# One transformer layer on one core: third to eighth row pairs also loaded with features first, and both input projections fed by sums and differences of the two row blocks

## Chip, cores and metric

One NeuronCore of one Trainium2 chip runs the whole program. The metric is the device time of one execution in microseconds (us). Time before: 2068.4 us, the median of 3 runs (2067.24 to 2069.75).

## What is computed

Two sequences (prompt and sample, 1024 rows of 1024 features, float32) pass through one encoder layer:

```python
mod = silu(c) @ w_ada + b_ada                 # shift, scale and gate, twice
h = rmsnorm(x, g_mix) * (1 + sc1) + sh1
z = h @ w_in                                  # 256 + 128 + 64 latents, 512 Fourier inputs
mla = attention(latents(z))                   # low-rank queries, keys, values
four = real(fft2(z[..., 448:])) @ w_four      # over rows and over 64 channels
x = x + ga1 * (concat(mla, four) @ w_out)
h2 = rmsnorm(x, g_ffn) * (1 + sc2) + sh2
x = x + ga2 * ((silu(h2 @ w_gate) * (h2 @ w_up)) @ w_down)
y = rmsnorm(x, g_final)
```

## The kernel before

Every float32 product is made of three matmuls. The helper `split` (L62 to L64) makes a rounded high part on ACT (L63, a cast) and the rest on DVE (L64, a subtraction); `mm3` (L78 to L81) multiplies high by high, high by low and low by high into one bank of PSUM.

The part that changes is the first stage and the transform stage behind it. The first stage goes through eight **row pairs**, four for each sequence; here they are counted from first to eighth (`k` = 0 to 7 in the code). A pair is two blocks of 128 rows, row block u = 0 and u = 1. The rows are stored so that row t of one block and of the other mirror each other in the Fourier transform over the rows. For each pair the program does this:

- `norm` loads the rows (tile `xt`, one row in each partition), sums their squares on ACT (L358, tile `junk`), takes 1/sqrt with six small POOL instructions (`rstd`, L102 to L109, tile `rs_r`), and scales the rows on DVE (L361).
- `flip` transposes 16 blocks of 128x128 on PE (L374), two chunks of features at a time, scales and shifts the result on its way out of PSUM (ACT, L381, tile `hf`, features in the partitions), and splits it into `hh` and `hl`.
- `zproj` (one for each row block) projects to the 448 latents, 24 matmuls with 448 columns from `hh`, `hl`; it then takes two more squares and `rstd`, applies the rotation (POOL adds, L426) and the norms (DVE, L427, L428), and stores the key part (`kv` to `ckv_d`). `latents` transposes the result (4 on PE, L442), splits it into `lh`, `ll` and stores these (`lat_d`).
- `evenodd` makes the sum and the difference of the two blocks on POOL (L396, tile `eo`) and splits them into `eoh`, `eol`. `fourier_in` multiplies these with weights into which the channel transform is folded (`wcs`, 280 and 256 columns), 24 matmuls each, and folds the results into `zc` and `zs`.

The order is written by hand: `pair(k)` runs both `zproj`, with the transposes of the next pair between them, then both `fourier_in` with the `latents` between, then `evenodd` of the next pair. The generator `extras` puts in one step at each `next(more)`: first eight chunks of the gate modulation (`wada`, 1 MB each, two buffers; 8 matmuls with 512 columns, L214), later the product of the output and Fourier weights (`wo4`, `lw`, L303), which goes to `wm_d` and `wn_d`. Each engine works through its queue in order, SyncE (SP) too, from whose queue all loads and stores here are issued: a store that waits for its data holds up the loads behind it.

The transform stage (`dft`, then `fourier_out`) splits the cosine and sine tables (`raw` to `tb`), `zc`, `zs` and the weights (`wraw` to `wm`, `wnr` to `wn`), multiplies, and stores to `fo_d`. It starts with `dft(0)`, for which the eighth pair of the first stage must be done. In between, chunks of the second modulation run (`mod2`). Attention and the FFN stand behind it and take most of the time.

## Time and profile before

| what | value |
|---|---|
| median of 3 runs | 2068.4 us |
| profiled execution, own time | 2068.6 us |
| its span in the profile | 2066.8 us |
| PE busy | 2018.9 us, 98% of the span |
| DVE, ACT, POOL busy | 68%, 43%, 41% |
| first pair's first projection starts | 51.1 us |
| second pair's projection starts | 75.1 us |
| transform stage: first `dft` matmul | 232.1 us |
| attention: first score matmul | 316.6 us |

The profile is of one execution. Times are counted from the span's start. "PE bank L81 <- DVE hl L64" in the view of waits means that a matmul of line 81 stood still until that DVE instruction ended. In the timeline a row has start, length, engine, line, operation, names of tiles, shapes and the number of instructions merged, and in brackets the idle time ahead of it. A matmul's length runs over into its successor (they are pipelined), so a matmul's price is read from one start to the next.

### The profile page before, as it was taken

Reading aid. Unit: us, or ns where it says so; the run is one execution under the profiler, and the core shown is the slowest. Engines: PE = TensorE matmul, PEld = TensorE weight load, DVE = VectorE, ACT = ScalarE, POOL = GpSimd, SP = SyncE. Lnnn points to the kernel's source line nnn. Section 1 sums busy time; section 2 is a strip of 40 time slices with the busy share of each in tenths; the row PEclk is TensorE's granted clock in tenths of the full one; section 3 lists DMA queues with packets and bytes.
Section 4 is the critical chain, followed back from the end, with each engine's and each line's share of the span. In section 5 each row is a group of like instructions: output and inputs, shape, how many; then the busy total and the mean of one; then the engine's idle time right before and its main releaser. Section 6 shows DMA issues by size and latency. Waiting matters only on the chain.

```text
span 2066.8 us, 28651 instructions
## 1 busy us (share of the span) xinstructions
PE 2018.9 (98%) x9994; PEld 1652.4 (80%) x9994; DVE 1406.0 (68%) x2078; ACT 898.4 (43%) x1753; POOL 841.4 (41%) x1014
## 2 busy tenths in 40 slices
PE   7899999999999999999999999999999999999998
PEld 4688778888888877888888888877788888888876
DVE  4567757766776778777777676778665665667685
ACT  2655535555555564232323355454333323336441
POOL 0555412111313227778778510333554454420142
PEclk9999999999999999999999999999999999999999
DMA  9675784533644375545545587665322222258662
GB/s 389 210 252 169 240 296 149 143 87 88 169 122 134 128 256 188 202 154 194 192 150 208 168 283 253 219 237 176 118 97 102 100 105 102 87 176 280 223 227 98
DMA packets 182685, 370.36 MB, mean 179 GB/s; under 512 B 18412, under 2 KB 57964, under 8 KB 179468
## 3 DMA queue, kind: packets, MB, share of 16 engines
q1 hardware_dynamic: 165196, 315.04, 45.0%
q0 software_dynamic: 17344, 53.49, 8.7%
q8 instruction: 78, 1.28, 0.3%
q14 instruction: 67, 0.55, 0.1%
HBM read 256.46 MB, written 120.39 MB: 182 GB/s over the span
## 4 chain that ended last, share of the span: by engine, by line
PE 55%; DVE 3%; DMA 2%; ACT 1%; POOL 1%; issue 1%; SPq 0%; DVEq 0%; ACTq 0%; POOLq 0%
PE bank L81 18%; PE bank L79 18%; PE bank L80 18%; DVE wl L64 1%; DMA draw<-t_d 1%; ACT wh L63 1%; DVE val L137 1%; DVE val L1599 0%; DMA val<-x_d 0%; DMA X<-hc_d 0%; DVE val L134 0%; DMA rgu<-in_wgu_dram 0%; DMA ga<-ga_d 0%; DMA draw<-s_d 0%; POOL rs_y L105 0%
## 5 line engine op out<-in xcount | busy, mean ns | idle before, releaser
L79 PE MATMUL bank<-H,wh 128*128 128x512 f32 x1232 | 487.6, 396 | 3.8 <-DVE val L137 1.9
L81 PE MATMUL bank<-H,wl 128*128 128x512 f32 x1232 | 488.4, 397 | 0.2 <-DVE wl L64 0.2
L80 PE MATMUL bank<-H,wh 128*128 128x512 f32 x1232 | 484.5, 393 | 0.3 <-DVE H L64 0.3
L79 PEld LDWEIGHTS bank<-H,wh 128*128 128x128 f32 x1232 | 231.3, 188 | 60.0 <-DVE val L137 2.8
L80 PEld LDWEIGHTS bank<-H,wh 128*128 128x128 f32 x1232 | 231.3, 188 | 57.9 <-DVE H L64 0.6
L81 PEld LDWEIGHTS bank<-H,wl 128*128 128x128 f32 x1232 | 231.3, 188 | 57.1 <-DVE wl L64 0.5
L64 DVE TENSOR_TENSOR wl<-draw,wh 128x512 fp32r<-128x512 f32 x286 | 201.9, 739 | 82.6 <-ACT wh L63 79.5
L137 DVE TENSOR_TENSOR val<-bank,val 128x512 f32<-128x512 f32 x200 | 136.6, 689 | 157.1 <-PE bank L81 151.6
L63 ACT CAST wh<-draw 128x512 fp32r<-128x512 f32 x286 | 168.8, 620 | 158.0 <-PE bank L80 91.4
L137 POOL TENSOR_TENSOR val<-val 128x512 f32<-128x512 f32 x58 | 83.5, 1447 | 367.0 <-DVE val L1573 189.2
L80 PE MATMUL bank<-wl,wh 128*128 128x512 f32 x572 | 223.7, 391 | 2.6 <-DVE wl L64 2.6
L63 ACT CAST wh<-rgu 128x512 fp32r<-128x512 f32 x172 | 106.8, 621 | 270.3 <-PE bank L80 210.8
L79 PE MATMUL bank<-wh 128*128 128x512 f32 x572 | 222.6, 389 | 0.0
L81 PE MATMUL bank<-wh,wl 128*128 128x512 f32 x572 | 222.6, 389 | 0.0
L63 ACT CAST wh<-val 128x512 fp32r<-128x512 f32 x133 | 82.3, 621 | 268.7 <-PE bank L80 249.2
L64 DVE TENSOR_TENSOR wl<-val,wh 128x512 fp32r<-128x512 f32 x133 | 133.5, 1005 | 78.1 <-ACT wh L63 77.9
L64 DVE TENSOR_TENSOR wl<-rgu,wh 128x512 fp32r<-128x512 f32 x172 | 164.3, 955 | 5.2 <-ACT wh L63 5.2
L134 POOL TENSOR_TENSOR val<-rgu 128x512 f32<-128x512 f32 x80 | 117.8, 1473 | 101.8 <-DMA rgu<-in_wgu_dram 98.0
L80 PEld LDWEIGHTS bank<-wl,wh 128*128 128x128 f32 x572 | 107.3, 188 | 28.6 <-DVE wl L64 6.4
L79 PEld LDWEIGHTS bank<-wh 128*128 128x128 f32 x572 | 107.4, 188 | 22.4
L81 PEld LDWEIGHTS bank<-wh,wl 128*128 128x128 f32 x572 | 107.4, 188 | 21.9
L1042 DVE TENSOR_REDUCE mx<-ps_s 128x1 f32<-128x1024 f32 x64 | 78.1, 1221 | 61.7 <-PE ps_s L1037 61.4
(356 smaller groups left out, 4113.0 us busy)
## 6 DMA issues: line engine op xcount, KB each, us to landing
rgu<-in_wgu_dram SPq DMA_DIRECT2D x86, 512.0 KB
draw<-s_d SPq DMA_DIRECT2D x143, 256.0 KB
s_d<-val POOLq DMA_DIRECT2D x88, 256.0 KB, 4.1
draw<-t_d SPq DMA_DIRECT2D x88, 256.0 KB
s_d<-val SPq DMA_DIRECT2D x66, 256.0 KB
draw<-in_w_down_dram SPq DMA_DIRECT2D x55, 256.0 KB
wada<-in_w_ada_dram SPq DMA_DIRECT2D x11, 1024.0 KB
xt<-in_x_dram SPq DMA_DIRECT2D x16, 512.0 KB
```

Of the source, the lines that this page charges most:

```text
L63: here["a"] = nc.scalar.copy(hi, src).ins
L64: here["v"] = nc.vector.tensor_tensor(out=lo, in0=src, in1=rd(hi), op=ALU.subtract).ins
L79: nc.tensor.matmul(out, lh, rh, start=first, stop=False, skip_group_check=cont)
L80: nc.tensor.matmul(out, lh, rl, start=False, stop=False, skip_group_check=cont)
L81: here["t"] = nc.tensor.matmul(out, ll, rh, start=False, stop=last, skip_group_check=cont).ins
L134: return eng.tensor_tensor(out=out, in0=x, in1=y, op=ALU.subtract).ins
L137: eng.tensor_tensor(out=out, in0=x, in1=y, op=ALU.add)
L1042: nc.vector.tensor_reduce(out=mx, in_=ps, axis=AX.X, op=ALU.max)
```

## The change

- `x` is also passed in transposed on the host (`xt0`, `xt1`: features first, 1 MB for each pair). From the third pair on this copy is loaded (`xT`) and the 16 transposes fall away. The rows are still loaded, for the squares alone; they are not scaled any more. In `scale_t` PE transposes the two columns `rs_r`, spread over 128 columns, so that a bank holds 1/sqrt along the free axis (2 transposes a pair); DVE multiplies `xT` with this bank (4 instructions of 128x512), and ACT scales and shifts in place (8 of 128x256).
- From the second pair on the latents use the same sum and difference as the Fourier inputs: `zboth` multiplies `eoh`, `eol` with the latent weights (48 matmuls with 448 columns, as before), and half the sum and half the difference of the two results are the two row blocks (one ACT copy, two DVE instructions). `hh`, `hl` and their splits fall away but for the first pair. The difference overwrites half of `hf` or `xT`; `eoh`, `eol` have two sets of buffers.
- `latents` of a pair run behind the next pair's `zboth`; the stores are collected and issued in `flush`. The next pair is prepared inside `zboth` (behind the first half in the second and third pair, behind 6 matmuls from the fourth on; the eighth pair already behind the sixth pair's first `fourier_in`).
- The seventh pair's `fourier_in` waits until `zboth` of the eighth has run. The splits of `zx`, `zc` and `zs` of the first sequence take their subtraction from POOL, not DVE. The loads of weights and of the second modulation, `prep_wm` and `stage3_loads` move.

```diff
-    def split(hi, lo, src):
+    def split(hi, lo, src, eng=None):
         here["a"] = nc.scalar.copy(hi, src).ins
-        here["v"] = nc.vector.tensor_tensor(out=lo, in0=src, in1=rd(hi), op=ALU.subtract).ins
+        here["v"] = (eng or nc.vector).tensor_tensor(out=lo, in0=src, in1=rd(hi), op=ALU.subtract).ins
 
...
+        EARLY = 7
+        nk = len(pairs)
...
+        def xt_load(k):
+            s, j = pairs[k]
+            st1["hf", k] = w.tile([P, NC, 2, P], F32, tag=("hh0", "hl0")[k % 2], name="xT")
+            nc.sync.dma_start(st1["hf", k], a[f"xt{s}"][j].rearrange("p (c u t) -> p c u t", c=NC, u=2))
...
+            squares(k, ms)
             r = rstd(ms, 2)
+            if k > 1:
+                st1["r", k] = r
+                return
             for u in range(2):
                 nc.vector.tensor_scalar(out=xt[u], in0=xt[u], scalar1=r[:, u : u + 1], scalar2=None, op0=ALU.mult)
+
+        def scale_t(k):
+            s, j = pairs[k]
+            hf = st1["hf", k]
+            r = st1.pop(("r", k))
+            rr = bank()[:, : 2 * P]
+            for u in range(2):
+                nc.tensor.transpose(rr[:, u * P : u * P + P], r[:, u : u + 1].broadcast_to([P, P]), ident)
+            for g in range(4):
+                h = hf[:, 2 * g : 2 * g + 2].rearrange("p c u t -> p c (u t)")
+                here["z"] = nc.vector.tensor_tensor(out=h, in0=h, in1=rr.unsqueeze(1).broadcast_to([P, 2, 2 * P]), op=ALU.mult).ins
+                for c in range(2):
+                    cc = 2 * g + c
+                    nc.scalar.activation(h[:, c, :], h[:, c, :], AF.Identity, bias=sh1[s][:, cc : cc + 1], scale=s1[s][:, cc : cc + 1])
 
         def flip(k, g):
...
-            eo = []
+            st1["eo", k] = []
+            if k % 2 == 1:
+                both = [w.tile([P, 2, NC, P], F32R, tag=f"h{t}1", name=f"eo{t}") for t in "hl"]
             for i, op in enumerate((ALU.add, ALU.subtract)):
-                f = w.tile([P, NC, P], F32, tag="eo", name="eo", bufs=1)
-                fh = w.tile([P, NC, P], F32R, tag=f"eoh{i}", name="eoh", bufs=1)
-                fl = w.tile([P, NC, P], F32R, tag=f"eol{i}", name="eol", bufs=1)
+                f = hf[:, :, 0, :] if i else w.tile([P, NC, P], F32, tag="eo", name="eo", bufs=1)
+                if k % 2 == 1:
+                    fh, fl = both[0][:, i], both[1][:, i]
+                else:
+                    fh = w.tile([P, NC, P], F32R, tag=f"eoh{i}", name="eoh", bufs=1)
+                    fl = w.tile([P, NC, P], F32R, tag=f"eol{i}", name="eol", bufs=1)
                 for g in range(2):
                     gs = slice(4 * g, 4 * g + 4)
                     with tc.issue_after(root) if root is not None and i == 1 else ExitStack():
                         nc.gpsimd.tensor_tensor(out=f[:, gs], in0=hf[:, gs, 0, :], in1=hf[:, gs, 1, :], op=op)
+                yield
+                for g in range(2):
+                    gs = slice(4 * g, 4 * g + 4)
                     split(fh[:, gs], fl[:, gs], f[:, gs])
-                    if i == 1 and k > 1:
-                        st1.setdefault(("odd", k), []).append(here["a"])
-                eo.append((fh, fl))
-            st1["eo", k] = eo
+                st1["eo", k].append((fh, fl))
+                yield
 
         def zproj(k, u):
...
+        def zboth(k, between):
+            eo = st1["eo", k]
+            pz = [bank() for _ in range(2)]
+            mz = tiny.tile([P, 4], F32, name="mz")
+            if 3 < k + 2 < nk:
+                norm(k + 2)
+            for i in range(2):
+                for c in range(NC):
+                    mm3(pz[i][:, :DZ], eo[i][0][:, c, :], eo[i][1][:, c, :], wz_h[:, c, :], wz_l[:, c, :], c == 0, c == NC - 1)
+                    if i == 0 and c in (1, NC - 1):
+                        between(c)
+            if k < 2 or k == nk - 1:
+                sk = [stile("lat") for _ in range(2)]
+            else:
+                if k == 2:
+                    st1["lat"] = w2.tile([P, 4, 512], F32, tag="hf", name="lat4", bufs=1)
+                sk = [st1["lat"][:, 2 * (k % 2) + u, :] for u in range(2)]
+            late_latents(k - 1)
+            nc.scalar.activation(sk[1][:, :DZ], pz[0][:, :DZ], AF.Copy, scale=0.5)
+            for u in range(2):
+                nc.vector.scalar_tensor_tensor(out=sk[u][:, :DZ], in0=pz[1][:, :DZ], scalar=(0.5, -0.5)[u], in1=sk[1][:, :DZ],
+                                               op0=ALU.mult, op1=ALU.add)
+            for u in range(2):
+                z_square(sk[u], mz[:, 2 * u : 2 * u + 2])
+            rz = rstd(mz, 4)
+            yield
+            for u in range(2):
+                z_out(k, u, sk[u], sk[u], rz[:, 2 * u : 2 * u + 2])
...
-                nc.sync.dma_start(ckv_d[s][i][:, ti, :], rd(kv[:, i, :]))
+                st1.setdefault("st", []).append((ckv_d[s][i][:, ti, :], rd(kv[:, i, :])))
             st1["sk", k, u] = sk
+            if k == 0:
+                flush()
+
+        def flush():
+            for dst, t in st1.pop("st", ()):
+                nc.sync.dma_start(dst, t)
 
...
+            xt_load(2)
+            x_load(3)
             fourier_in(0, 1)
-            evenodd(1, root2)
+            for _ in evenodd(1):
+                pass
+            norm(2)
+
...
+        def late_latents(k):
+            if k > 0:
+                latents(k, 0)
+                if k + 1 < nk:
+                    here["l0"] = here["a"], here["v"]
+                latents(k, 1)
 
         def pair(k):
             if k == 0:
                 return first_pair()
-            zproj(k, 0)
+            if k + 2 < nk:
+                xt_load(k + 2)
+            if k + 3 < nk:
+                x_load(k + 3)
+            if k > 2:
+                next(more, None)
+
+            def prepare(kk):
+                scale_t(kk)
+                st1["steps"] = evenodd(kk)
+                next(st1["steps"])
+
+            def between(c):
+                if k + 1 < nk and c == (1 if k > 2 else NC - 1) and k + 1 < EARLY:
+                    prepare(k + 1)
+                    if k < 2:
+                        norm(k + 2)
+                if c == 1:
+                    flush()
+                else:
+                    if k + 1 < nk:
+                        next(st1["steps"], None)
+                        next(st1["steps"], None)
+                    if k < 4:
+                        next(more, None)
+
+            z = zboth(k, between)
+            next(z, None)
             if k + 1 < nk:
-                flip(k + 1, 0)
-                flip(k + 1, 1)
+                next(st1["steps"], None)
             next(more, None)
-            zproj(k, 1)
-            latents(k, 0)
-            here["l0"] = here["a"], here["v"]
-            if k + 1 < nk:
-                flip(k + 1, 2)
-                flip(k + 1, 3)
-            if k + 2 < nk:
-                x_load(k + 2)
-            next(more, None)
-            fourier_in(k, 0)
-            latents(k, 1)
-            next(more, None)
-            fourier_in(k, 1)
-            if k + 2 < nk:
-                norm(k + 2)
-            if k + 1 < nk:
-                evenodd(k + 1, here["p"])
+            for i in range(2) if k + 2 != nk else ():
+                fourier_in(k, i)
+                if i == 0:
+                    if EARLY <= k + 2 < nk:
+                        prepare(k + 2)
+                    next(more, None)
+                    with tc.issue_after(here["z"]):
+                        next(z, None)
+            next(z, None)
 
         for k in range(nk - 1):
...
+        z = zboth(nk - 1, lambda c: flush() if c == 1 else None)
+        next(z)
+        flush()
+        with behind():
+            split(zxs[0], zxs[1], zx, nc.gpsimd)
+            z0 = zcos_split(0, nc.gpsimd)
         wm0 = wm_half(0, 0, 0, wr)
-        pair(nk - 1)
-        with tc.issue_after(here["l0"][0]), tc.issue_after(here["l0"][1]):
+        wm1 = wm_loads(0, 0, 1), wn_load(0, 0, raw_tile("wnr")[:, :512])
+        next(z, None)
+        fourier_in(nk - 2, 0)
+        with behind():
+            nc.scalar.copy(tcor, cor[:, :NTE])
             for c in range(2):
                 split(tb[0][0][:, c, :], tb[0][1][:, c, :], raws[0, c])
+        fourier_in(nk - 2, 1)
+        late_latents(nk - 1)
+        fourier_in(nk - 1, 0)
+        with behind():
+            nyq_split()
+        fourier_in(nk - 1, 1)
+        flush()
...
-                    split(zsin[0][:, c : c + 2], zsin[1][:, c : c + 2], zs[s][:, c : c + 2, :])
+                    split(zsin[0][:, c : c + 2], zsin[1][:, c : c + 2], zs[s][:, c : c + 2, :], nc.gpsimd if s == 0 else None)
...
+            if s == 0:
+                with behind():
+                    here["ny"] = here["a"], here["v"]
+                    halves = [wm0, wm_half(0, 0, 1, w, wm1[0])]
+                    wms[0] = {0: (halves, next(wn0))}
+            if mid:
+                mid()
...
-                abn = dft(1)
-                prep_wm(1)
-                mod_vecs(mr, bank2, bT, gT, 24, 1, s2, sh2)
-                early.close()
-                E3 = ExitStack()
-                e = E3.enter_context(tc.tile_pool(name="p3e", bufs=1, side="left", reuse_waits="tile"))
-                rc, rs = stage3_loads()
+
+                def last_mod():
+                    mod2(NC - 1)
+                    nc.vector.tensor_copy(mr, chunks.pop("ps"))
+
+                prep_wm(1, [0], wmr)
+                abn = dft(1, last_mod)
+                prep_wm(1, [1])
...
+    def across(x):
+        return x.reshape(2, 4, P, NC, P).transpose(1, 4, 3, 0, 2).reshape(4, P, NC * 2 * P)
```

What the instruction order shows at three places. First TensorE around the projection of a pair in the middle of the stage (`xt` rows, `lat` latents, `wada`/`scT` modulation, `wz` latent weights); before:

```order
L81 MATMUL bank<-wz_h,hl 128x448
L374 MATMUL bank<-ident,xt 128x128 x8
L214 MATMUL bank<-wada,scT 32x512 x4
L79 MATMUL bank<-wz_h,hh 128x448
L80 MATMUL bank<-wz_l,hh 128x448
```

And now, in a later pair of the same kind, where `rs_r` is the column of 1/sqrt:

```order
L79 MATMUL bank<-wz_h,eoh 128x448
L80 MATMUL bank<-wz_l,eoh 128x448
L81 MATMUL bank<-wz_h,eol 128x448
L384 MATMUL bank<-ident,rs_r 128x128 x2
L79 MATMUL bank<-wz_h,eoh 128x448
```

Two groups of 8 transposes a pair became one group of 2, and the projection reads `eoh`, `eol` in place of `hh`, `hl`.

Second, ScalarE ahead of the second pair's projection; before:

```order
L63 CAST kv<-lat 128x128
L358 ACTIVATE junk,ms<-xt 128x1024
L63 CAST hh<-hf 128x512
L358 ACTIVATE junk,ms<-xt 128x1024
L381 ACTIVATE hf<-bank,sh_0_75,s_0_73 128x256 x2
L63 CAST lh<-bank 128x512
L63 CAST hh<-hf 128x512
L381 ACTIVATE hf<-bank,sh_0_75,s_0_73 128x256 x3
```

And now, from the first evictions of that pair on:

```order
L411 ACTIVATE hf<-bank,sh_0_75,s_0_73 128x256 x2
L63 CAST kv<-lat 128x128
L411 ACTIVATE hf<-bank,sh_0_75,s_0_73 128x256 x2
L63 CAST lh<-bank 128x512
L411 ACTIVATE hf<-bank,sh_0_75,s_0_73 128x256 x4
L63 CAST lh<-bank 128x512
L63 CAST eoh<-eo 128x512 x2
L63 CAST eoh<-hf 128x512 x2
L363 ACTIVATE junk,ms<-xt 128x1024 x2
```

The third pair's squares (`junk,ms`) have moved behind the second pair's evictions and the casts of its sum and difference.

Third, the DMA queue of SP at the end of the first stage (`raw` tables, `wraw` and `wnr` weights of the transform, `lat_d` and `ckv_d` stores of latents); before:

```order
L630 DMA raw<-in_tcos_dram 128x514 x2
L630 DMA raw<-in_tsin_dram 128x512 x2
L634 DMA raw<-in_tcor_dram 128x258
L651 DMA wraw<-wm_d_85 128x512 x6
L433 DMA ckv_d_96<-kv 128x128
```

And now, behind the same tables:

```order
L510 DMA lat_d_93<-ll 512x1x128
L510 DMA ckv_d_96<-kv 128x128
L510 DMA ckv_d_97<-kv 128x128
L510 DMA ckv_d_96<-kv 128x128
L510 DMA ckv_d_97<-kv 128x128
L510 DMA lat_d_92<-lh 512x1x128
L510 DMA lat_d_93<-ll 512x1x128
L510 DMA lat_d_92<-lh 512x1x128
L510 DMA lat_d_93<-ll 512x1x128
L768 DMA wraw<-wm_d_85 128x512 x4
L762 DMA wnr<-wn_d 48x512
```

The weight loads `wraw` stood ahead of the last latents' stores; they now stand behind nine of them (the first of `ll`, four of `kv`, four of `lh` and `ll`), and `wnr` behind `wraw`.

More of the change, by code (lines that the diff above doesn't have):

```diff
@@ L414, in zproj, with z_out @@
                                               scale=1.0 / math.sqrt(KVL), accum_out=mz[:, 1:2]).ins
[L415 to L419 removed]
+        def z_out(k, u, pz, sk, rz):
+            s, j = pairs[k]
+            ti = 4 * u + j
             kp = pz[:, QL + KVL : DZ]
@@ L643, in zcos_split, with nyq_split, wn_load @@
             return z
-        z0 = zcos_split(0)
-        def wm_half(s, g, h, pool):
+        zn = [wr.tile([P, 4, NY2], F32R, name=f"zn{i}") for i in range(2)]
+        def nyq_split():
+            for s in range(2):
+                ss = slice(NNYQ * s, NNYQ * s + NNYQ)
+                split(zn[0][:, :, ss], zn[1][:, :, ss], zc[s][:, :, NCOS:])
+        def wn_load(s, g, wnr):
+            nc.gpsimd.memset(wnr, 0.0)
+            nc.sync.dma_start(wnr[:NY2], wn_d[:, 512 * g : 512 * g + 512])
+            return wnr
@@ new lines, in prep_loads, with prep_wm @@
+        def prep_loads(s, g):
+            wnr = wn_load(s, g, w.tile([P, 512], F32, tag="wnr", name="wnr", bufs=2))
+            return wnr, [wm_loads(s, g, h) for h in range(2)]
+        def prep_wm(s, gs, ready=None):
+            wms.setdefault(s, {})
+            for g in gs:
+                wnr, raw = ready or prep_loads(s, g)
+                with ExitStack() as st:
+                    if s == 0:
+                        for ins in here["ny"]:
+                            st.enter_context(tc.issue_after(ins))
+                    halves = [wm_half(s, g, h, wr if (g, h) == (0, 0) else w, raw[h]) for h in range(2)]
+                    wms[s][g] = halves, list(prep_wn(s, g, wnr))[1]
```

193 lines of the change are left out of this document (103 added, 90 removed).

## Prediction

> **What bounds the kernel now.** I read the page first, then a table of stretches, then who waits for whom on PE, then the timeline around those waits.
>
> ```profile
> span 2066.8 us, 28651 instructions
> PE 2018.9 (98%) x9994; PEld 1652.4 (80%) x9994; DVE 1406.0 (68%) x2078; ACT 898.4 (43%) x1753; POOL 841.4 (41%) x1014
> ```
>
> PE is busy for 98% of the span, so what PE no longer has to do comes off the end, and so does a stretch in which PE stands still. The profiled execution took 2068.6 us itself, 0.2 above the median; I take the sum from 2068.6. The stretches (length, then busy time of each engine, granted PE clock, DMA share, GB/s) tell where PE stands in the stages that change:
>
> ```profile
> core 0: us, PE busy (x) PEld busy (x) DVE busy (x) ACT busy (x) POOL busy (x), PEclk, DMA share, GB/s
> 64.60:72.00 7.40, 4.00 (x34) 2.71 (x32) 3.66 (x13) 4.05 (x13) 5.03 (x16) 1.00 0.07 22
> 76.90:80.00 3.10, 0.00 (x0) 0.00 (x0) 3.10 (x4) 3.10 (x8) 1.64 (x2) 1.00 0.65 199
> 80.00:84.20 4.20, 4.18 (x13) 3.77 (x14) 3.57 (x6) 0.18 (x1) 0.55 (x1) 0.59 0.55 163
> 84.20:88.20 4.00, 1.77 (x13) 1.41 (x11) 2.15 (x5) 2.62 (x8) 2.54 (x4) 1.00 0.99 312
> 104.00:126.00 22.00, 22.00 (x147) 18.09 (x146) 12.85 (x32) 13.66 (x34) 12.07 (x26) 1.00 0.85 269
> 193.90:214.00 20.10, 18.77 (x123) 17.42 (x122) 14.09 (x30) 12.20 (x32) 11.27 (x23) 1.00 0.34 110
> 214.00:232.10 18.10, 17.09 (x106) 15.70 (x105) 11.99 (x28) 9.41 (x27) 10.06 (x21) 1.00 0.70 226
> 232.10:240.00 7.90, 7.90 (x68) 7.90 (x67) 7.62 (x20) 5.13 (x14) 0.00 (x0) 1.00 1.03 281
> ```
>
> In a middle pair (104 to 126) PE never stands, and DVE, ACT and POOL are busy for 12 to 14 of 22 us: there only fewer PE instructions help. PE stands at the second pair's start, in the last two pairs, and at the transform's start. The views of waits of 72 to 100 us and of 100 to 250 us name the releasers:
>
> ```profile
> PE bank L81 <- DVE hl L64: 3.1, 1, 3.1
> PE bank L214 <- DMA wada<-in_w_ada_dram: 2.2, 1, 2.2
> ```
>
> ```profile
> PE bank L442 <- DVE lat L427: 1.6, 3, 0.9
> PE bank L442 <- DVE lat L428: 0.8, 1, 0.8
> ```
>
> **Step 1, the transposes.** The group has all of them from the third pair on; two rows of the timeline give the price from one start to the next:
>
> ```profile
> L374 PE MATMUL bank<-ident,xt 128*128 128x128 f32 x96 | 12.4, 272 | 0.0
> ```
>
> ```profile
> 109.28 1.03 PE L374 MATMUL bank<-ident,xt 128*128 128x128 f32 x8
> 110.25 1.06 PE L214 MATMUL bank<-wada,scT 128*32 128x512 f32 x8
> ```
>
> Eight take 110.25 - 109.28 = 0.97 us, 0.121 each. 96 go and 6 x 2 transposes of `rs_r` come, of the same shape: 84 x 0.121 = **-10.2**. The 48 projection matmuls stay 48. What hides the rest in a middle pair: DVE loses the row scaling and the `hl` splits and gains four products and two combinations, about as much; ACT loses four casts and gains one copy; POOL loses one `rstd`. With PE at 20 us all stay under 15. An edit that costs nothing here would cost its length if PE were not the last.
>
> **Step 2, the second pair's start.** Now:
>
> ```profile
> 75.07 0.37 PE L79 MATMUL bank<-wz_h,hh 128*128 128x448 f32 x1
> 76.52 0.37 PE L80 MATMUL bank<-wz_l,hh 128*128 128x448 f32 x1
> 80.02 0.47 PE L81 MATMUL bank<-wz_h,hl 128*128 128x448 f32 x1 [3.14 <-DVE hl L64]
> ```
>
> Seven starts in 1.45 us: 0.207 a matmul. PE then stands 3.1 us, and in the next 4.2 us its clock is granted at 0.59: 4.2 x 0.41 = 1.7 more, 4.8 in all. Page and trace agree on why: the Trainium skill, "TensorE: Matmul & The Clock Gate", Part 1, says that the array falls to half its clock after an idle window of about 3.4 us and needs as long to come back; by it the waits of about 1 us that I find below cost nothing further.
>
> Now the same place after the change, with the durations of these rows:
>
> ```profile
> 68.34 0.69 DVE L64 TENSOR_TENSOR eol<-eo,eoh 128x512 fp32r<-128x512 f32 x1
> 68.14 1.03 ACT L381 ACTIVATE hf<-bank,sh,s 128x256 f32<-128x256 f32 x2
> 70.72 0.30 ACT L63 CAST kv<-lat 128x128 fp32r<-128x128 f32 x1 [1.55 <-DVE lat L428]
> 72.48 1.06 ACT L358 ACTIVATE junk<-xt 128x1024 bf16<-128x1024 f32 x1
> 74.44 0.57 ACT L63 CAST lh<-bank 128x512 fp32r<-128x512 f32 x1
> 73.72 0.22 POOL L102 TENSOR_SCALAR rs_v<-ms 128x2 f32<-128x2 f32 x1 [3.26 <-ACT junk L358]
> 75.64 0.20 POOL L109 TENSOR_TENSOR rs_r<-rs_w,rs_y 128x2 f32<-128x2 f32 x1
> 75.79 1.29 POOL L396 TENSOR_TENSOR eo<-hf 128x512 f32<-128x512 f32 x1
> ```
>
> The first pair's difference now lies in `hf` itself, so the second pair's evictions can't start before its last split is read, at 69.0 (68.34 + 0.69) in place of 68.1. ACT in its new order: two evictions to 70.0, the `kv` cast to 71.0 (it still waits for its row until 70.7), two evictions to 72.0, `lh` to 72.6, four evictions to 74.6, `lh` to 75.2, then the casts `eoh`. POOL has the first half of the sum at 72.0 + 1.29 = 73.3, a difference at 74.6, the other sum at 75.9, the other difference at 77.2. So the first `eoh` is there at 75.8, the first `eol` 0.69 later at 76.5; the second ones by 77.2, in time. PE, ready at 75.1, runs its third matmul at 76.5 in place of 75.5: 1.0 late. Its first half ends at 76.5 + 22 x 0.207 = 81.1. There stand the two transposes of the third pair's `rs_r`. Its squares now come after the casts (77.8) and end at 79.9; `rstd` takes 75.84 - 73.72 = 2.1: 82.0, so PE waits 0.9. What is queued behind those transposes on PE is the second half of the projection, and nobody but PE waits for that. Step 2: -4.8 + 1.0 + 0.9 = **-2.9**.
>
> **Step 3, the modulation chunk.**
>
> ```profile
> 82.57 1.98 SPq L204 DMA_DIRECT2D wada<-in_w_ada_dram  x3
> 88.21 1.07 PE L214 MATMUL bank<-wada,scT 128*32 128x512 f32 x8 [2.24 <-DMA wada<-in_w_ada_dram]
> ```
>
> The chunk's last half was issued at 82.6, behind stores, and landed 5.6 us later; PE stood 2.2 us. SP now reaches the load behind the last `ll` store, at about 76, so it lands near 82; PE comes to it at 82.0 + 0.25 + 0.4 = 82.7. Between a gain of all 2.2 and of nothing (if the 1 MB `xT` behind it shares the queues, 3.3 us at 312 GB/s) I take **-2.0**.
>
> **Step 4, the last two pairs.** The `latents` transposes wait for the norm of the row block that has just been projected: 1.6 + 0.8 us. One pair later these rows have been ready for over 10 us. **-2.4**; it is zero if the norms slip by a pair.
>
> **Step 5, the transform's start.** From its first matmul (232.14) to the first modulation:
>
> ```profile
> 240.00 0.39 PE L79 MATMUL bank<-wm,A 128*128 128x512 f32 x1
> 240.23 0.39 PE L80 MATMUL bank<-wm,A 128*128 128x512 f32 x1
> 245.69 1.06 PE L907 MATMUL bank<-wada,scT 128*32 128x512 f32 x8
> ```
>
> `dft` takes 7.9 us, and 13 matmuls at 0.23 take 3.0: 10.9 of 13.6, so 2.7 are lost. The change keeps PE on both last pairs' `fourier_in` after the eighth projection (14 us from its end T), but the order of SP puts `wraw` behind the last pair's latent stores. ACT, which copied nothing ahead this time, passes two squares, four `kv` and four `lh` casts and the splits of `zx`, `zc` and `tb` first; by the rows' 0.3 and 0.6 us the last `ll` is ready at about T + 14.7. Loads of this kind took this long:
>
> ```profile
> 217.89 7.18 SPq L651 DMA_DIRECT2D wraw<-wm_d  x6
> 222.25 1.28 ACT L63 CAST wm<-wraw 128x512 fp32r<-128x512 f32 x2 [0.26 <-DMA wraw<-wm_d]
> 233.56 1.09 SPq L843 DMA_DIRECT2D wnr<-wn_d  x2
> 240.53 0.62 ACT L845 CAST wnh<-wnr 128x512 fp32r<-128x512 f32 x1 [2.53 <-DMA wnr<-wn_d]
> ```
>
> 4.4 us for `wraw` (T + 19), up to 7.0 for `wnr` (issued near T + 17). Behind them on ACT stand the splits of `zs`, of the sine table and of `A`, and PE waits for all three: the sine half of `dft` ends near T + 25.5 in place of 22, and the 19 matmuls behind it end near T + 30.4, 4.2 us over T + 14 + 7.9 + 19 x 0.23. A second price at this place: POOL now subtracts for `zx`, `zc` and `zs`, 1.3 us each, and two DVE splits run beside it. Bounds: 0 (loads in time) to 4.2 + 2.5 (`wnr` at its 7.0) + 1.7 (the clock falls as in step 2). Step 5: 4.2 - 2.7 = **+1.5**, from -2.7 to +5.7.
>
> **Sum.** -10.2 - 2.9 - 2.0 - 2.4 + 1.5 = -16.0; 2068.6 - 16.0 = 2052.6, 2052.4 by the median. I say **2053**. The attention and the FFN keep their order, so the gain passes on.
>
> **Rivals.**
> - *The waits only move.* The transposes' 10.2 come off, and steps 2 to 4 return at the `rs_r` transposes, at `xT` or at the transform: 2068.6 - 10.2 = 2058.4. For it: ACT and DVE queues are tight in steps 2 and 5. Against: a middle pair has no wait now. 24%.
> - *All waits go.* Steps 2 to 5 at their best: 10.2 + 4.8 + 2.2 + 2.4 + 2.7 = 22.3: 2046.3. 9%.
> - *`xT` isn't there.* The DMA engines are used for 0.85 of the 22 us of a middle pair, 18.7 us; 1 MB more at that rate (269/0.85 = 316 GB/s) is 3.3: 22.0 against the 20 that PE now wants. Three pairs with modulation chunks at 2.0 are 6: 2058.6. Against: the loads start in a stretch with a share of 0.07 to 0.65, and latent stores move out of it. 8%.
> - *Slower: the preparation outlasts its cover.* From the `rs_r` transposes on, a product (0.7), four evictions (2.0), POOL's four (5.2), the last cast and split (1.3), with the order's waits about 13 us; PE gives 42 x 0.207 + 0.9 + 6.1 = 15.7 before the next projection. If it took 18.7, PE would stand 3.1 us and run 1.7 behind at the lower clock, six times: 6 x 4.8 = 29: 2081. It decides from 16 us on. For it:
>
> ```profile
> 77.96 1.46 POOL L396 TENSOR_TENSOR eo<-hf 128x512 f32<-128x512 f32 x1 [0.88 <-ACT hf L381]
> 78.21 1.75 DVE L64 TENSOR_TENSOR hl<-hf,hh 128x512 fp32r<-128x512 f32 x1
> ```
>
> A DVE split beside a POOL add took 1.75 in place of 0.69. The Trainium skill, "GPSIMD Engine Reference", section 1, says that POOL shares its SBUF interfaces with DVE when that reads two SBUF inputs; these rows agree, and by the rule all four splits of a pair would take 1.75, the chain 17.3, and the time 6 x 1.6 more, 2062. Against: four slow splits are 4 x 1.06 = 4.2 more only if none overlaps with ACT, and half of them are due a half projection later. 11%.
>
> **How the numbers follow.** Forecast (2049 to 2056) 46%, the rivals 24, 9, 8 and 11%, and 2% for no change. A run tells 0.2% (4.1 us) from none. Faster holds the forecast and the first three rivals less a few per cent of tails: 0.83; same 0.06; slower 0.11. The range 2045 to 2062 leaves out the slower rival, no change and the tails.
>
> **What would show it.** L374 falls to 32 instructions. Step 2: the wait ahead of the first L81 with `eol` falls to about 1 us and the clock stays at 1.00; the transposes of `rs_r` wait about 1 us once. Step 3: no wait on `wada` over 0.5. Step 4: no wait on `lat`. Step 5: PE waits for `tb`, `zsin` or `A` soon after the first `dft` matmul, 4 us in all. I am wrong if PE waits at the start of the third to seventh projection, or for `xT`, or if the transform's start costs over 8 us.

## The result, and the profile after

The changed kernel takes 2059.65 us (median of 6 runs, 2056.97 to 2061.09), the kernel before 2069.97 us beside it: ratio 0.9951, 95% interval 0.9938 to 0.9964. It is faster, by 10.3 us where 16.0 were forecast; the time lies inside the stated range (2045 to 2062), 6.7 us above its likeliest value and 3.7 above the band of the forecast itself (2049 to 2056). The profiled execution took 2061.09 us itself, 7.5 less than the profiled one of before.

The head of its page:

```profile
span 2059.3 us, 28434 instructions
PE 2006.8 (97%) x9910; PEld 1641.9 (80%) x9910; DVE 1397.6 (68%) x2071; ACT 890.2 (43%) x1732; POOL 831.9 (40%) x977
```

PE has 84 instructions fewer and is busy 12.1 us less, but its share fell from 98 to 97%: some of what it no longer does is now waiting. The stretches that answer to those of before (length, busy time of each engine, granted PE clock, DMA share, GB/s) show where:

```profile
core 0: us, PE busy (x) PEld busy (x) DVE busy (x) ACT busy (x) POOL busy (x), PEclk, DMA share, GB/s
76.60:80.00 3.40, 3.40 (x18) 3.08 (x18) 3.35 (x7) 2.81 (x5) 0.82 (x1) 1.00 0.96 283
80.00:84.40 4.40, 2.94 (x19) 1.36 (x17) 0.56 (x3) 1.11 (x4) 1.74 (x6) 1.00 1.01 404
104.10:126.00 21.90, 21.56 (x141) 16.82 (x141) 12.44 (x26) 16.25 (x39) 14.46 (x27) 1.00 0.83 315
202.80:215.70 12.90, 12.90 (x108) 12.80 (x107) 7.30 (x21) 8.61 (x26) 6.67 (x13) 1.00 0.78 222
215.67:220.24 4.57, 1.14 (x8) 0.73 (x6) 4.51 (x9) 0.27 (x1) 3.46 (x4) 0.99 0.26 80
220.24:226.11 5.87, 5.87 (x36) 5.75 (x37) 1.76 (x3) 3.21 (x6) 1.36 (x2) 0.71 1.03 310
226.11:230.69 4.58, 3.37 (x26) 2.98 (x25) 4.58 (x11) 3.63 (x13) 4.48 (x4) 1.00 0.61 180
230.69:238.40 7.71, 6.45 (x28) 4.54 (x26) 7.71 (x15) 5.89 (x11) 0.43 (x1) 1.00 0.93 340
```

The second pair (76.6 to 84.4) keeps its clock, where 0.59 was granted before. The last two pairs run through. The first `dft` begins at 215.67, 16.5 us earlier than before, and then everything stops: PE is busy for 1.14 of 4.57 us, runs at 0.71 of its clock for the next 5.87, and waits again. It ends at 230.69, after 15.0 us in place of 7.9. From the first `dft` matmul to the first score matmul (308.00) it is 92.3 us, 84.5 before. Behind that, the rest of the span is 1751.3 us, 1750.2 before: attention and FFN pass on what reaches them.

So the profile's account is short: -0.2 (start of the first projection), -16.3 (first stage), **+7.8** (transform stage), +1.1 (behind it) = -7.5, each term rounded. PE's waits from 72 to 300 us:

```profile
PE bank L79 <- DVE zs L546: 2.5, 1, 2.5
PE bank L80 <- DVE tb L64: 2.0, 2, 1.1
PE bank L384 <- POOL rs_r L109: 1.5, 1, 1.5
PE bank L1054 <- DMA wada<-in_w_ada_dram: 1.3, 1, 1.3
PE bank L145 <- DVE modrow L1110: 1.0, 1, 1.0
PE bank L81 <- DVE eol L64: 0.6, 1, 0.6
PE bank L214 <- DMA wada<-in_w_ada_dram: 0.3, 1, 0.3
```

Of these, 4.5 us (`zs`, `tb`) belong to the first `dft`, 1.3 to the first chunk of the second modulation right behind it. The rows of DVE, ACT, PE and SP there:

```profile
207.74 0.35 DVE L494 TENSOR_SCALAR lat<-lat,rs_r 128x256 f32<-128x256 f32 x1 [3.38 <-POOL rs_r L109]
208.92 0.30 ACT L63 CAST kv<-lat 128x128 fp32r<-128x128 f32 x1 [3.69 <-DVE lat L495]
213.80 3.39 DVE L64 TENSOR_TENSOR tb<-raw,tb 128x514 fp32r<-128x514 f32 x2 [1.92 <-ACT tb L63]
217.24 0.39 PE L80 MATMUL bank<-tb,zh 128*128 128x258 f32 x1 [0.94 <-DVE tb L64]
220.24 0.58 PE L79 MATMUL bank<-tb,zh 128*128 128x256 f32 x1 [2.50 <-DVE zs L546]
229.19 0.33 SPq L1033 DMA_DIRECT2D wq_l<-wq_d  x1
230.99 1.38 SPq L1059 DMA_DIRECT2D wada<-in_w_ada_dram  x3
```

DVE and ACT stand 3.4 and 3.7 us at the last pair's norms (`rs_r` is still on POOL); the splits of `zx`, `zc` and `tb` are queued behind them. Then two `tb` splits take 3.39 us on DVE while POOL subtracts for `zc`, and the additions for `zs`, which free the bank that PE wants, stand behind those.

### The profile page after: what moved, and what is told of

The parts are those of the page before. It is cut to its first block, busy times and chain, and to the rows that moved or that the text cites. A ratio compares the mean times of both kernels' runs of the same rounds, so it can differ in the third digit from the quotient of the medians.

```text
span 2059.3 us, 28434 instructions
## 1 busy us (share of the span) xinstructions
PE 2006.8 (97%) x9910; PEld 1641.9 (80%) x9910; DVE 1397.6 (68%) x2071; ACT 890.2 (43%) x1732; POOL 831.9 (40%) x977
## 4 chain that ended last, share of the span: by engine, by line
PE 55%; DVE 3%; DMA 2%; POOL 1%; issue 1%; SPq 0%; ACT 0%; DVEq 0%; ACTq 0%; POOLq 0%
PE bank L81 19%; PE bank L80 19%; PE bank L79 18%; DVE wl L64 1%; DMA draw<-s_d 1%; DMA draw<-t_d 1%; DVE val L137 1%; DMA val<-x_d 0%; POOL val L137 0%; DVE val L1760 0%; DMA X<-hc_d 0%; ACT wh L63 0%; DVE val L134 0%; POOL rs_y L105 0%; SPq L1719 0%
## 5 line engine op out<-in xcount | busy, mean ns | idle before, releaser
L80 PEld LDWEIGHTS bank<-wl,wh 128*128 128x128 f32 x572 | 107.3, 188 | 29.4 <-DVE wl L64 7.4
L79 PEld LDWEIGHTS bank<-wh 128*128 128x128 f32 x572 | 107.4, 188 | 23.4 <-ACT wh L63 0.9
```

What stands on the lines that cost most here:

```text
L79: nc.tensor.matmul(out, lh, rh, start=first, stop=False, skip_group_check=cont)
L80: nc.tensor.matmul(out, lh, rl, start=False, stop=False, skip_group_check=cont)
```

## The experiments

T is the end of the eighth projection on PE (202.0 us in the changed kernel); the columns are lengths from the profiles. `t_same` is the changed kernel once more. Medians and ratios are each against the kernel before, timed beside it (2069.8 to 2071.2).

| run | median, ratio (95%) | T to first `dft` | first `dft` | wait at first chunk | T to issue of chunks | T to first score |
|---|---|---|---|---|---|---|
| changed | 2059.65, 0.9951 (0.9938-0.9964) | 13.7 | 15.0 | 1.3 | 29.0 | 106.0 |
| t_same | 2060.09, 0.9950 (0.9936-0.9965) | 13.7 | 15.1 | 1.3 | 29.4 | 107.7 |
| t_dve | 2059.80, 0.9943 (0.9931-0.9955) | 13.7 | 13.0 | 0.9 | 27.5 | 103.3 |
| t_loads | 2058.87, 0.9939 (0.9927-0.9952) | 13.7 | 15.6 | 0 | 29.7 | 105.1 |
| t_both | 2061.77, 0.9956 (0.9944-0.9969) | 13.7 | 14.2 | 1.4 | 28.2 | 106.9 |
| t_flips | 2072.97, 1.0007 (0.9998-1.0016) | 18.5 | 7.9 | 0.8 | 23.9 | 105.0 |
| t_first | 2061.63, 0.9949 (0.9932-0.9965) | 15.1 | 9.2 | 5.8 | 28.1 | 107.5 |
| t_nolat | 2065.70, 0.9971 (0.9961-0.9981) | 19.8 | 10.3 | 0 | 27.2 | 107.9 |
| t_late | 2060.79, 0.9951 (0.9939-0.9964) | 13.7 | 15.3 | 0 | 29.2 | 106.1 |
| t_firstlate | 2061.63, 0.9955 (0.9942-0.9969) | 15.1 | 8.9 | 0 | 27.8 | 106.2 |
| t_firstgate | 2057.53, 0.9933 (0.9918-0.9949) | 15.5 | 8.9 | 2.7 | 23.4 | 104.6 |
| **t_all** | **2054.59, 0.9930 (0.9916-0.9943)** | 15.1 | 9.4 | 0.1 | 21.1 | 102.1 |
| t_alllate | 2060.22, 0.9962 (0.9949-0.9975) | 15.1 | 9.4 | 0 | 21.2 | 106.5 |

The columns behind the median come from one profiled execution each. Changed and t_same are the same kernel and differ by 1.7 us in the last one, so a difference of that size there says nothing.

**What holds the first `dft`?** Two theories, one edit each, and both together. `t_dve`:

```diff
-            split(zxs[0], zxs[1], zx, nc.gpsimd)
-            z0 = zcos_split(0, nc.gpsimd)
+            split(zxs[0], zxs[1], zx)
+            z0 = zcos_split(0)
```

(and the same for `zsin`).

> The changed kernel with one thing undone: the subtractions of the splits of zx, zc and zs of the first sequence are back on DVE. Theory A (the transform's weights are late because their loads stand behind the latents' stores on SP): little, 0 to -1.5 us against the changed kernel, and PE still waits and runs at a low clock in the first dft. Theory B (DVE works slower beside POOL's subtractions, 1.7 us for a tb split of 128x514, and everything behind it on DVE is late: the zs additions that free PE's bank, and the ll split whose store holds up the loads): the two tb splits take about 0.7 us each, PE's waits of 0.94 and 2.50 us in the first dft go and with them the 1.7 us at the low clock, -4 to -6 us, about 2054 to 2056.

`t_loads`:

```diff
+        raw0 = wm_loads(0, 0, 0)
         z = zboth(nk - 1, lambda c: flush() if c == 1 else None)
         next(z)
-        flush()
...
-        wm0 = wm_half(0, 0, 0, wr)
+        wm0 = wm_half(0, 0, 0, wr, raw0)
         wm1 = wm_loads(0, 0, 1), wn_load(0, 0, raw_tile("wnr")[:, :512])
+        flush()
```

> The changed kernel with the transform's weight loads moved on SP: the first two wraw ahead of the eighth projection, the other two and wnr ahead of the sixth... seventh pair's latents' stores. Theory A (loads behind stores): the first dft gets back the 4.2 us of the forecast, about 2055.5. Theory B (DVE is held up by POOL): only the wait for the sine half goes (1.2 us), the 3.4 us of waits and 1.7 us of low clock at the start of the first dft stay: -1 to -2 us, about 2058.

`t_both` has both edits.

> Both edits together. If A and B each hold a part: the first dft takes 8 to 9 us in place of 15.0 and the time is 2052 to 2053. If a third cause holds it up (ACT's queue of casts, which copied nothing ahead), less than 3 us come back and PE waits for ACT casts.

The `tb` splits of `t_dve`:

```profile
212.82 1.30 DVE L64 TENSOR_TENSOR tb<-raw,tb 128x514 fp32r<-128x514 f32 x2 [1.92 <-DMA ckv_d<-kv]
```

With POOL quiet two of them take 1.30 us in place of 3.39. The `dft` is 2.0 us shorter, and the median is where it was, not the 4 to 6 us lower that B forecast: B names a real price, a small one. PE now waits for other subtractions of DVE in the same place (1.5 us for `zh`, 1.4 for `zs`). Theory A falls: with the weights' loads ahead of the stores the `dft` takes as long as ever (15.6), and 0.8 to 1.2 us in the median is no more than these runs tell from nothing. Together they bring 0.8 and no time: in `t_both` PE waits 3.3 us for `zh`, because the weights' splits, ready sooner, have moved ahead of those of `zx` and `zc` in DVE's queue. Less than 3 us came back, as the third cause of that expectation would have it, but PE waits for DVE there, not for ACT's casts.

**The transposes by themselves.** `t_flips` puts the 16 transposes of a pair back, with DVE scaling the rows; `xT` is not loaded, and the rows' loads move:

```diff
-            nc.sync.dma_start(st1["hf", k], a[f"xt{s}"][j].rearrange("p (c u t) -> p c u t", c=NC, u=2))
...
-            for u in range(2):
-                nc.tensor.transpose(rr[:, u * P : u * P + P], r[:, u : u + 1].broadcast_to([P, P]), ident)
+                for c in range(2):
+                    for u in range(2):
+                        cc = 2 * g + c
+                        nc.tensor.transpose(pt[:, c, u, :], xt[u][:, cc * P : (cc + 1) * P], ident)
```

> The changed kernel with the features-first copy not used: from the third pair on the rows are scaled on DVE and transposed on PE again (16 a pair in place of 2), everything else as changed. Forecast's price: 84 x 0.121 = 10.2 us more, about 2070. Rival (PE's transposes lie in waits that the new order has anyway): under 5 us more. Rival (the longer chain through PE, PSUM and ACT makes PE wait at each pair): 15 us or more.

It is 13 us slower than the changed kernel, about as slow as the one before. Of the first stage, the second pair's start to the first `dft` takes 158.5 us in place of 140.6. One group of transposes, and the one that replaced it in the changed kernel:

```profile
148.32 1.91 PE L384 MATMUL bank<-ident,xt 128*128 128x128 f32 x16
```

```profile
137.41 0.38 PE L384 MATMUL bank<-ident,rs_r 128*128 128x128 f32 x2
```

From start to the next matmul's start they take 1.66 and 0.14 us, so six pairs cost 9.1 (10.2 forecast). The other 8.8 us are in the main waits that come back (2.7 for scaled rows, 1.7 for a chunk, 3.3 for the last pair's `lat`, where the changed kernel waits 2.4 in all) with the lower clock behind them. In exchange the first `dft` takes 7.9 us again: it starts at T + 18.5 in place of 13.7, and while PE waits 3.3 us for `lat` and runs at a low clock (0.65 from 226 to 229.5 us), ACT and DVE catch up. In this kernel less work on PE moves the wait to where the other engines' work is due.

**Order or amount?** `t_first` changes only the order:

```diff
+        raw0 = wm_loads(0, 0, 0)
+        split(zxs[0], zxs[1], zx)
+        z0 = zcos_split(0)
         z = zboth(nk - 1, lambda c: flush() if c == 1 else None)
         next(z)
-        flush()
-        with behind():
-            split(zxs[0], zxs[1], zx, nc.gpsimd)
-            z0 = zcos_split(0, nc.gpsimd)
-        wm0 = wm_half(0, 0, 0, wr)
-        wm1 = wm_loads(0, 0, 1), wn_load(0, 0, raw_tile("wnr")[:, :512])
-        next(z, None)
         fourier_in(nk - 2, 0)
-        with behind():
-            nc.scalar.copy(tcor, cor[:, :NTE])
-            for c in range(2):
-                split(tb[0][0][:, c, :], tb[0][1][:, c, :], raws[0, c])
+        nc.scalar.copy(tcor, cor[:, :NTE])
+        for c in range(2):
+            split(tb[0][0][:, c, :], tb[0][1][:, c, :], raws[0, c])
+        wm1 = wm_loads(0, 0, 1), wn_load(0, 0, raw_tile("wnr")[:, :512])
+        flush()
+        with behind():
+            next(z, None)
         fourier_in(nk - 2, 1)
-        late_latents(nk - 1)
         fourier_in(nk - 1, 0)
         with behind():
             nyq_split()
+        late_latents(nk - 1)
         fourier_in(nk - 1, 1)
+        with behind():
+            wm0 = wm_half(0, 0, 0, wr, raw0)
         flush()
```

(and `zsin` on DVE, as in `t_dve`).

> The changed kernel itself once more, as the yardstick for the runs beside it: about 2059.7, first dft 15 us, transform stage 92.

> The changed kernel with another order at the transform's start, no work added or left out: the splits of zx, zc and the cosine table stand ahead of the last pair's norms on ACT and DVE (subtractions on DVE), its latents ahead of its second Fourier input, the splits of wm behind them, the first two wraw loads ahead of the eighth projection. Theory C (head of line: ACT and DVE stand 3.4 to 3.7 us at the last pair's norms, which wait for 1/sqrt from POOL, with the transform's splits queued behind them): the first dft takes 8 to 9 us in place of 15.0, the stage 86 to 87 in place of 92, the time 2053 to 2055. Theory D (not the order but the amount of DVE's work between the last projection and the dft): the first dft stays above 12 us and the time at 2058 or more.

> The changed kernel without the last pair's latents: rotation, norms, splits and the 8 transposes of the eighth pair are left out (zeros are stored); the sums of its rows and 1/sqrt still run. Theory C: nothing stands ahead of the transform's splits any more, the first dft takes 9 to 10 us, the time falls by 5 to 7 us, 0.9 of it the transposes. Theory D: only the DVE work that goes (four norms of 0.3, four kv splits of 0.25, two of 0.7: 3.6 us) comes off: dft 11 to 12. If neither (the tables or weights are late from DMA): dft stays above 13.

`t_first` settles C against D. `t_both` has the same subtractions on DVE and its first loads ahead too, and its first `dft` takes 14.2 us; with the new order it takes 9.2, 5.0 less, though it starts 1.4 later. But the time did not move (C forecast 2053 to 2055). The wait had a second gate behind it; PE's wait and SP's rows of `t_first`:

```profile
PE bank L1055 <- DMA wada<-in_w_ada_dram: 5.8, 1, 5.8
```

```profile
219.03 2.62 SPq L510 DMA_DIRECT2D ckv_d<-kv  x4
221.70 2.59 SPq L510 DMA_DIRECT2D lat_d<-lhl  x4
228.67 0.33 SPq L1034 DMA_DIRECT2D wq_l<-wq_d  x1
230.47 1.38 SPq L1060 DMA_DIRECT2D wada<-in_w_ada_dram  x3
```

SP issues the last latents' stores until 224.3 (5.2 us for these eight), then stands 4.4 us until they have landed, since `wq_l` takes over their memory; the chunks stand behind `wq_l`. PE comes 5.8 us early and waits for the first chunk in place of the splits. `t_nolat`, which leaves out the last pair's norms, splits and transposes of the latents and stores zeros, settled nothing: it was 6.0 us slower than the changed kernel where C forecast 5 to 7 faster. With the latents gone the weights' casts came ahead of the tables' on ACT and held these up,

```profile
220.36 1.30 ACT L63 CAST wm<-wraw 128x512 fp32r<-128x512 f32 x2 [8.15 <-DMA wraw<-wm_d]
```

which is the same blocking of a queue, by another instruction: PE waits 6.9 us for `tb`.

**The second gate.** `t_late` and `t_firstlate` (with the order of `t_first`) let PE come later to the chunks:

```diff
-                    if t > 0:
-                        mod2(t - 1)
+                    if t > 2:
+                        mod2(t - 3)
...
-                abn = dft(1, last_mod)
+                mod2(5)
+                abn = dft(1, lambda: mod2(6))
+                mod2(NC - 1)
+                nc.vector.tensor_copy(mr, chunks.pop("ps"))
```

> The changed kernel with the second modulation's chunks two steps later on PE (the first one behind the fourth piece of the transform's output in place of the second; the last one behind the second dft); nothing else. Theory E (two gates side by side: the splits on ACT and DVE hold the first dft, and the loads of the modulation chunks, which wait on SP for the last latents' stores, hold the first chunk; the wait at one is cover for the other): alone this gives back only the 1.3 us that PE still waits for the first chunk, 2058 to 2060.

> The new order of the splits (as in the run that brought the first dft to 9.2 us) and the later modulation chunks together. Theory E: both gates are open, PE waits less than 1 us at the first chunk, the stage takes 84 to 86 us in place of 92 to 94, the time is 2052 to 2055. Rival F (the wait only moves on: to the last chunk, to the weights of the second half or to attention's loads): the stage stays above 90 us and the time at 2058 or more.

E is half right. Alone, the later chunks bring next to nothing, as it said. With both together, rival F holds: the transform's second weights, loaded behind the chunks, are late, the stage from the first `dft` to the first score takes 91.0 us and the time is 2061.63.

```profile
PE bank L79 <- ACT wm L63: 3.8, 1, 3.8
```

That points to what the gate is: neither the chunks nor the weights, but the moment from which SP can issue any of them. `t_firstgate` moves that moment, keeping the order of `t_first`:

```diff
-        flush()
+        flush(nc.gpsimd)
...
         zsplit(0, z0)
-        nc.sync.dma_start(rd(wq_l), wq_d)
...
             zsplit(1)
+        nc.sync.dma_start(rd(wq_l), wq_d)
```

> The new order of the splits as in t_first (first dft 9.2 us) and, with it, the loads behind the stage let go earlier: the last pair's latents are stored from POOL's queue, so that SP reaches the modulation chunks without standing behind these stores, and the load of wq_l, which waits until the last stores have landed because it takes over their memory, stands behind the chunks and the second weights. Theory G (in all kernels so far the stage ends 75 to 81 us behind the issue of the chunk loads, since the chunks and second weights behind them come from one queue that waits for the last stores): the chunks are issued near 219 us in place of 230, PE waits for none of them, the stage takes 83 to 86 us in place of 92 to 94 and the time is 2051 to 2055. Rival H (3 MB of chunks so early take the DMA engines from the tables and first weights): the first dft goes above 11 us or the first weights are late, and the time stays at 2058 or more.

`t_all` also loads `wnr` ahead of the eighth projection; `t_alllate` adds the later chunks.

```diff
         raw0 = wm_loads(0, 0, 0)
+        wnr0 = wn_load(0, 0, raw_tile("wnr")[:, :512])
...
-        wm1 = wm_loads(0, 0, 1), wn_load(0, 0, raw_tile("wnr")[:, :512])
+        wm1 = wm_loads(0, 0, 1), wnr0
```

> As t_firstgate, and the load of wnr moved ahead of the eighth projection: there SP stood 4.2 us at this load, because the memset of its tile stood on POOL behind the last latents' stores. Theory G: the three modulation chunks are issued near 220.5 us after the start in place of 225.9, the wait for the first chunk falls from 2.7 us to below 1, the stage from 89.1 to 85 to 87 us, the time from 2057.5 to 2054 to 2056. Rival H (the DMA engines and not the issue set the arrival): the wait stays near 2.7 and the time at 2057 to 2058.

> As t_all, with the modulation chunks two steps later on PE as in t_firstlate. Theory G: with the second weights issued by 226 us, the wait of 3.8 us that t_firstlate had for them is gone too; the stage takes 84 to 86 us and the time is 2053 to 2055. If H holds, PE waits for the second weights again (over 2 us) and the time is that of t_firstgate, 2057 to 2058, or more.

The chunks go out at T + 23.4 and T + 21.1 in place of T + 28.1; the wait for the first falls from 5.8 to 2.7 and to 0.1, and the median from 2061.6 to 2057.5 and **2054.6**. SP and the largest wait from 205 to 300 us in `t_all`:

```profile
222.77 2.44 SPq L1060 DMA_DIRECT2D wada<-in_w_ada_dram  x3
```

```profile
PE bank L145 <- DVE modrow L1112: 1.0, 1, 1.0
```

`t_all` beats both kernels: its five runs lie from 2052.31 to 2055.80, the eleven of the changed kernel from 2056.97 to 2063.41 (on other chips, where the kernel before took the same within 0.5 us). By the ratios the step from the changed kernel (0.9951, 0.9950) to `t_all` (0.9930) is about 4 us, with intervals that just overlap; the step from `t_firstgate` (0.9933) to `t_all` can't be told from nothing that way, and rests on the traces. H falls: the first `dft` stays at 8.9 and 9.4 us, and the wait goes. G's mechanism holds, its numbers only in part: in `t_firstgate` the chunks went out at 225.9, not 219, because SP stood at the load of `wnr`, and the time was 2057.5, not 2051 to 2055; `t_all` came as forecast in time (2054.6, with 87.0 us from the first `dft` to the first score), its chunks at 222.8 in place of 220.5; `t_alllate`, forecast at 2053 to 2055, took 2060.2. There the second weights are in time, as G said, but the last two chunks meet the second `dft`, and PE waits 3.6 us for chunks and 2.5 for `modrow`: later chunks are harmful once the loads are early. The second gate alone, taken away without the new order of the splits, was not run. The busy share of the DMA engines, in 40 slices of 1 us from 205 to 245, tells the same without any PE row. The changed kernel:

```profile
DMA  0689969999920039999999940799788999999999
GB/s 16 198 260 195 183 205 367 347 289 320 312 81 0 0 112 259 270 309 337 349 328 298 305 154 0 203 369 336 196 272 360 401 426 426 451 401 328 340 334 387
```

And `t_all`:

```profile
DMA  1968999998999999999999999999999999999999
GB/s 34 249 237 225 326 345 302 345 339 216 283 315 350 318 300 282 298 269 264 308 259 378 360 401 434 401 426 422 301 338 342 424 410 381 401 264 252 422 426 391
```

In the changed kernel the engines stand still around 217 and 229 us although megabytes are still to be loaded: at 217 SP stands at a store whose `ll` leaves DVE only at 218.4, at 229 it has just been let go by the last stores (the row of `wq_l` at 229.19). The edit of `t_firstgate` took two things of `t_first` out of the way of the chunks: the 5.2 us in which SP issues the last eight stores, which POOL now does, and the 4.4 us in which it waits for them ahead of `wq_l`, which now stands behind the chunks. No run parts the two. The Trainium skill, "DMA: Bandwidth & Descriptors", section "Issuing engines are not separate DMA queues", says that issuing from several engines only saves the sequencer's time to start a DMA, usually small. The 5.2 us are time of this kind, and here they stood ahead of loads that PE waited for.

## Why the prediction was right in the first stage and wrong at the transform's start

- **Step 1, the transposes, -10.2: right.** In the changed stretch (75.1 us to the first `dft`) the groups of L374 took 13.37 us from start to start, 2.24 of it the wait for `wada`; the twelve transposes of `rs_r` take 1.05. That is -10.1. `t_flips` prices them at 9.1.
- **Step 2, the second pair, -2.9: right, -2.2 measured.** The walk through the queues held: the first split was forecast for 76.5 us and PE's matmul went on at 76.33; the wait for `rs_r` is 1.46 in place of 0.9. 2.7 us are lost in place of 1.9, and the clock stays at 1.00.
- **Step 3, `wada`, -2.0: right, -1.9.** 0.3 of 2.2 us is left.
- **Step 4, `lat`, -2.4: right, -2.3.** No wait on `lat` is left behind the first pair.
- **Steps 1 to 4: -17.5 forecast, -16.5 measured** (157.07 to 140.57 us).
- **Step 5, the transform's start, +1.5 (-2.7 to +5.7): wrong, +7.8 measured, outside its own bounds.** This term is most of the miss: of the 8.5 us between the forecast's 16.0 and the 7.5 of the profiled executions it is 6.3, steps 1 to 4 are 1.0, and 1.1 came behind the transform, where nothing was forecast. The first `dft` alone costs 7.2 more; 1.0 is won back up to the first chunk (1.7 us are lost there over 26 matmuls, 2.7 over 13 before). That is +6.2 for the stretch that the working covers, outside its bounds too. 1.7 are lost later (1.0 of it at `modrow`: the second `dft` no longer lies between its copy and the transposes that read it). The working charged 4.2 us to `wraw` and `wnr` behind the stores on SP; `t_loads` shows that this price was not paid there: without the stores ahead of them the `dft` is no shorter. The step that failed is the walk through ACT's queue: it let the splits of `zx`, `zc` and `tb` run without a pause behind the `kv` casts, while in fact ACT and DVE stood 3.7 and 3.4 us ahead of those, at norms that wait for POOL's 1/sqrt; that the order costs the `dft` its time is what `t_first` shows (14.2 to 9.2 us). POOL's subtractions, the "second price", were named, but stand neither in the sum nor in the bounds: 2.0 us of the `dft` in `t_dve`. The low clock behind the waits, 1.7 in the bounds, came true: 5.87 x 0.29 = 1.7.
- **What the working had no row for:** the chunks and second weights behind the last stores. Step 5 walked SP's queue only as far as `wnr`. That queue holds a second gate at nearly the same time, so that removing the first (`t_first`) gave nothing. With both gone, `t_all` lies 15.2 us under its kernel before by the medians, 14.5 by the ratio; the forecast was 16.0, but for a kernel without these edits.
- **Rivals.** "The waits only move" (2058.4) is what came, in time and in kind: the transposes' 10.1 came off, and the 6.4 us of steps 2 to 4 went again at the transform, one of the three places that it named. That the time still lies inside the stated range is luck as far as the forecast's own sum goes: the range was wide enough for this rival. "All waits go" (2046.3) was not reached by any run. "`xT` isn't there": no PE instruction waits for it; DVE does, 4.3 us in all, under cover of PE's work. "The preparation outlasts its cover": no projection from the third on waits, with the DVE splits of the sums at 1.03 us on average, though the longest (1.82) reaches the 1.75 of its worst case. The expected sign of failure, a transform's start that costs over 8 us, nearly came: 7.8.

## What to carry to other kernels

When PE loses work ahead of a change of stage, walk every engine's queue, SP's too, from the last instruction that is moved to the first load of the next stage but one, and look for the instruction that waits longest: its wait is passed on to what is queued behind it (here 3.4 us on DVE, 3.7 on ACT, 4.4 on SP in `t_first`). Where one wait goes and the time stays, look for a second gate at the same moment before the theory is given up; here taking away the first alone gained nothing. A DMA share that falls to zero while loads are outstanding, as at 217 and 229 us here, points to the issuing queue.

## What the runs showed of the hardware

PE's clock fell without a long idle time. In `t_dve` two waits of 1.53 and 1.42 us, with four matmuls between them, were followed by 3.2 us at half clock:

```profile
core 0: us, PE busy (x) PEld busy (x) DVE busy (x) ACT busy (x) POOL busy (x), PEclk, DMA share, GB/s
214.69:219.03 4.34, 1.39 (x9) 0.80 (x7) 4.28 (x11) 0.27 (x1) 2.04 (x3) 0.97 0.78 220
219.03:222.20 3.17, 3.17 (x15) 3.05 (x16) 1.33 (x3) 1.96 (x4) 0.00 (x0) 0.50 0.98 318
```

In the changed kernel waits of 0.94 and 2.50 us within 4.57 us were followed by 3.17 us at 0.50. Behind single waits the granted clock stayed at 1.00: 1.46 us in the second pair of the changed kernel, 2.24 at the chunk of the kernel before (88.21 us), 2.67 at the chunk of `t_firstgate`. The prediction's sentence that waits of about 1 us cost nothing further held for these single waits; two close together cost the clock in both traces, and what exactly is counted the runs do not show. The Trainium skill, "TensorE: Matmul & The Clock Gate", Part 1, speaks of idle windows of about 3.4 us; in the stretch of `t_dve` above PE was busy for 1.39 of 4.34.
